# A pool of small tiles opened first, and the low parts of one product loaded into seven stage buffers

## The chip, the cores and the metric

The kernel runs on one core of a Trainium2 chip. The metric is the device time of one execution in microseconds (us). TensorE (PE in the profile) does the matmuls; VectorE (DVE), ScalarE (ACT) and GpSimd (POOL) do the element-wise work; SyncE (SP) issues most loads. DMA transfers are issued by SP, ACT and POOL.

## The reference

Two layers of a decoder trunk on 1024 tokens of width 1024, all in float32. In each layer a normalised input goes through one input projection of 3072 columns, whose parts feed a causal depthwise convolution of 31 taps (512 channels) and a retention of 4 heads; their outputs, side by side, go through the output projection `w_out` and are added to the residual. Then comes the squared-ReLU MLP (1024 to 4096 and back), then a gated per-layer input:

```
for i in range(DEPTH):
    z = rms_norm(x, norm_mix_g[i]) @ w_in[i]
    ...
    mix = jnp.concatenate([conv_out, ret_out], axis=-1) @ w_out[i]
    x = x + mix
    h = rms_norm(x, norm_ffn_g[i])
    x = x + jnp.square(jax.nn.relu(h @ w_ff1[i])) @ w_ff2[i]
    h = rms_norm(x, norm_ple_g[i])
    x = x + jax.nn.sigmoid(h @ w_ple_gate[i]) * (p[i] @ w_ple_proj[i])
return rms_norm(x, final_norm_g)
```

## The kernel before

The residual x lies transposed in SBUF for the whole run, in the pool `const`: 8 blocks of 128 channels by 2 halves of 512 tokens. Half 0 and half 1 of the tokens go through most products one after the other.

Every product is done in three matmuls (`mm3`, L252 to L254). A float32 number is split into a high part, cast by ACT to the type that TensorE takes whole (L220), and a low part, the remainder by DVE (L221); the product is high by high, high by low, low by high. So each weight tile (128 x 1024, 512 KB) exists as a `stage` tile (as loaded, by SP at L225), a `w_hi` and a `w_lo` tile, each of these pools with two buffers. `gemm` runs over eight blocks of 128 channels, 24 matmuls of 512 columns for one weight tile. The matmul's moving operand is the activation (high or low part, in `h`, `hx`, `form` or `pp`), its weights are 128 columns of `w_hi`, `w_lo` or, in the MLP's paired products, of `s_hi`, `s_lo`.

The weights of the input and output projection are used twice, once for each half. At the first use the low part is also stored to DRAM (`low_...`, L246), and at the second it is loaded back by SP into `w_lo` (L240) rather than computed again; only the cast to `w_hi` (L241) is left of the split.

The place that the change speaks of is the start of the MLP's part in each layer, which is where the output product of half 1 runs. There the code opens pools over the memory that the convolution's pools have left: `at`, `hx`, `s_hi` and `s_lo` with two buffers each, and inside them `ft` with seven. Then, in program order:

- seven fillers (`PRE` = 7, `ff1_half`): half-products of the first MLP matrix for half 0, which give PE work while the convolution of half 1 ends. Each copies a PSUM tile into an `at` buffer (ACT L602), adds the second half-product (DVE L605), applies ReLU and square (ACT L606, L607) and stores the tile to DRAM (`early`, issued by ACT at L608). An `at` buffer is free again when its store has landed;
- `w_out` of half 1 for output blocks 0 to 3, eight blocks in all, each with one weight tile whose low part was kept;
- sums and splits for the first paired MLP product (`ff1_sums`, `ff1_parts`: loads into `stage`, then DVE L588 to L591 into two `ft` buffers, ACT L220 and DVE L221 into `s_hi` and `s_lo`);
- `w_out` for blocks 4 to 7, then the norm of half 1 (`norm_forms`), which needs all of them, and which takes `ft` buffers again.

After these the paired products of the first MLP matrix run (530 to 750 us in layer 0, 1702 to 1925 us in layer 1), then those of the second (756 to 1030 and 1932 to 2200 us). A Winograd-like form is used there: sums of weight blocks are the weights, in `s_hi` and `s_lo`, and sums of activations the moving operand.

The order of the instructions on each engine is set by the tile framework's scheduler, which takes program order with priorities (`background` moves work in the order). The framework also places the pools: a pool's buffers lie at one address in all 128 partitions, one pool behind the other in the order in which they are opened; pools opened inside a `with` are given back when it ends and others take their place. The wait that a reused buffer brings is put in by the framework.

Of the kernel before, what the change touches and what calls it, by code (L numbers as in the profile page):

```python
# [13 lines left out]
F32R = mybir.dt.float32r  # L14
# [4 lines left out]
P = 128  # L19
D = 1024  # L20
# [3 lines left out]
HT = 512  # L24
# [48 lines left out]
class _Trunk:  # L73
    def __init__(self, ctx, tc, x, xT, pT, pos, wts, vecs, convw, tabs, outT):
        self.tc, self.nc = tc, tc.nc
        self.x_tok, self.xT, self.pT, self.pos, self.wts = x, xT, pT, pos, wts
        self.vecs, self.convw, self.tabs, self.outT = vecs, convw, tabs, outT
        pool = lambda name, bufs, **kw: ctx.enter_context(tc.tile_pool(name=name, bufs=bufs, **kw))
        psum = bass.MemoryType.PSUM
        self.const = pool("const", 1)  # L80
        self.pools = {
            "stage": pool("stage", 2),
            "w_hi": pool("w_hi", 2),
            "w_lo": pool("w_lo", 2),
            "h": pool("h", 8),
            "tmp": pool("tmp", 2),
            "small": pool("small", 3),
            "ps_mm": pool("ps_mm", 5, space=psum),
            "ps_ret": pool("ps_ret", 2, space=psum),
            "ps_aux": pool("ps_aux", 1, space=psum),  # L90
        }

        self.small([P, 1], "pad")
        self.right = ctx.enter_context(ExitStack())
        self.norm_pools()
        self.dram = pool("dram", 1, space=bass.MemoryType.DRAM)
        self.low = {}
# [130 lines left out]
    def weight(self, L, t):  # L228
        first = bool(self.next_weights)
        st = self.next_weights.pop(0) if first else self.stage_weight(L, t)  # L230
        hi, lo = self.tile("w_hi", D, F32R), self.tile("w_lo", D, F32R)
        kept = self.low.get((L, t))
        with ExitStack() as order:
            if first:
                for ins in self.gates.pop(0):
                    order.enter_context(self.tc.issue_after(ins))
            else:
                order.enter_context(self.background(-URGENT))
            if kept is not None:
                self.nc.sync.dma_start(out=lo.bitcast(F32), in_=kept)  # L240
                self.nc.scalar.copy(hi, st)  # L241
            else:
                self.split(st, hi, lo)
        if t < T_FF1 and kept is None:
            kept = self.dram.tile([P, D], F32, name=f"low_{L}_{t}")
            self.nc.gpsimd.dma_start(out=kept, in_=lo.bitcast(F32))  # L246
            self.low[L, t] = kept
        return hi, lo
# [344 lines left out]
    def block(self, p):  # L593
        return 4 * (p // 2) + p % 2

    def ff1_half(self, L, p, hs, early, w=None):
        nc = self.nc
        w = w or self.weight(L, T_FF1 + self.block(p))
        t = self.ft("at")
        n = KB // 2  # L600
        ps = self.gemm(w, (hs[0][:n], hs[1][:n]))
        nc.scalar.copy(t[:, 0, :], ps)  # L602
        ps = self.gemm(w, (hs[0][n:], hs[1][n:]), n)
        r = t[:, 1, :]
        nc.vector.tensor_add(r, ps, t[:, 0, :])  # L605
        nc.scalar.activation(r, r, AF.Relu)  # L606
        nc.scalar.activation(r, r, AF.Square)  # L607
        nc.scalar.dma_start(out=early[p // 2][:, p % 2], in_=t)  # L608
# [256 lines left out]
    def run(self):  # L865
# [8 lines left out]
        for L in range(DEPTH):  # L874
# [12 lines left out]
            with self.stage_pools(gen=16, conv_acc=4, ret=4, ctmp=3, rtmp=2, u=3):  # L887
                if L > 0:
                    norm_b()
                hs = h1[0]  # L890
# [18 lines left out]
                hs = h1[1]  # L909
# [10 lines left out]
                kept = self.dram.tile([P, KB, HT], F32, name=f"kept_{L}")  # L920
                h2 = self.norm(0, v0 + V_FFN, 0, True, keep=kept)
# [5 lines left out]
            early = [self.dram.tile([P, 2, 2, HT], F32, name=f"early_{L}_{j}") for j in range(NFB)]  # L927
# [23 lines left out]
            with self.stage_pools(at=2, hx=2, s_hi=2, s_lo=2):  # L951
                with self.stage_pools(ft=7):
                    for p in range(PRE):
                        self.ff1_half(L, p, h2, early)
                    mix = (mB[0] + rB[0], mB[1] + rB[1])
                    self.w_out(L, 1, mix, range(4))
                    with self.background(-URGENT):
                        fa, fb, _ = self.ff1_sums(L, 0)
                        sa, sb = self.ff1_parts(fa), self.ff1_parts(fb)
                    self.w_out(L, 1, mix, range(4, KB))  # L960
                    t2, t1 = rB[2], mB[2]
                    t3 = [self.pools["hx"].tile([P, 4, HT], F32R, name="hx") for _ in range(2)]
                    late = self.norm_forms(1, v0 + V_FFN, SLACK, kept, t1, t2, t3)
                    e = self.early_load(0, early, "tmp")
                    for p in range(PRE, NPAIR - 1):
                        self.ff1_half(L, p, h2, early)
                    w = self.weight(L, T_FF1 + self.block(NPAIR - 1))
                    raw = self.tile("stage", D)[:, HT:]
                    nc.sync.dma_start(out=raw, in_=self.wts[L * NTILES + T_FF1 + self.block(0) + 2, :, HT:])
                    with self.background(-URGENT):  # L970
                        ws = self.ff1_plain(raw), sa, sb
                    self.ff1_half(L, NPAIR - 1, h2, early, w)
                    q22, t4 = (h2[2][0], h2[3][0]), (h2[2][1], h2[3][1])
                    for f, i in ((q22, 0), (t4, 1)):
                        for item in late:
                            self.split(item[i], *item[2](f))
                    now = ws, e
                    self.ring = [*t2, *t1, t3[0], *q22, t3[1], None, *t4]
                    self.turn, self.coming = 0, []
                    for p in range(NPAIR):  # L980
                        now = self.ff1_pair(L, p, (t1, t2, t3, t4, q22), *now, early, forms, hook)
                with self.stage_pools(form=1, acc=2):
                    self.ring[8] = self.pools["form"].tile([P, 4, HT], F32R, name="form")
                    f = self.ff2_pairs(L, sources)
                    self.norm_pools()
                    self.merge_pairs(0)
                    self.ff2(L, NFB - 1, 0, f[:2])
                    self.merge_pairs(1)
                    h3A = self.norm(0, v0 + V_PLE, SLACK)
                    self.ff2(L, NFB - 1, 1, f[2:])  # L990
# [94 lines left out]
```

## Time and profile before

| | |
|---|---|
| median of 3 runs | 2378.33 us (2377.74 to 2378.8) |
| the profiled execution's own time | 2378.69 us |
| its span, first to last instruction | 2376.7 us |
| mean granted TensorE clock | 0.994 |
| PE busy | 2314.1 us, 97% of the span, 10548 matmuls |
| DVE busy | 1857.8 us, 78% |
| ACT busy | 1267.6 us, 53% |
| DMA | 403.29 MB, 170 GB/s mean |

PE busy is the union of the matmuls' times from issue to the modelled end, and consecutive matmuls overlap: a 512-column matmul is shown with some 390 ns, while the next one starts some 230 ns after it. PE's pace in a stage without idle time is therefore read from the start times in the timeline, not from the mean duration. In a timeline the square brackets behind a row give the time that the engine stood idle before it and what ended that time.

### The profile page before, as it was taken

To read this page: it belongs to the slowest core of one execution; us is meant where nothing else is said; L and a number is where in the kernel's file an instruction comes from. 1 tells how busy PE (TensorE), PEld (TensorE's weight loads), DVE (VectorE), ACT (ScalarE), POOL (GpSimd) and SP (SyncE) were. 2 spreads that over 40 slices of the span, in tenths; PEclk is the share of its full clock that TensorE was granted. 3 is DMA by queue.
4 is the path that set the end of the run, shared out by engine and by line. 5 is a ranking of instruction groups with operands and counts; after the bars stand their busy time and mean duration, and the time that the engine had idled before them with its cause. 6 is when DMAs were issued, how large, how long until landed. Compare 5 with 4: busy or idle time off the path is not lost.

```text
span 2376.7 us, 29537 instructions
## 1 busy us (share of the span) xinstructions
PE 2314.1 (97%) x10548; PEld 1886.0 (79%) x10548; DVE 1857.8 (78%) x3262; ACT 1267.6 (53%) x2090; POOL 231.9 (10%) x364
## 2 busy tenths in 40 slices
PE   8999999999999999999999999999999999999998
PEld 7887887778887878788888888777788877777887
DVE  8999997376666677878999889845766667777788
ACT  5335237365556676736542352464655567676454
POOL 1000011001221101000000100100022111010000
PEclk9999999999999999999999999999999999999999
DMA  7644544666666444422265454555566654343324
GB/s 271 194 160 150 172 149 163 227 199 204 219 233 239 141 151 138 155 72 88 89 195 180 149 171 156 175 196 187 191 218 233 237 194 164 126 162 120 89 80 151
DMA packets 119171, 403.29 MB, mean 170 GB/s; under 512 B 13216, under 2 KB 21408, under 8 KB 119024
## 3 DMA queue, kind: packets, MB, share of 16 engines
q1 hardware_dynamic: 64032, 220.75, 30.5%
q0 software_dynamic: 43472, 157.59, 18.6%
q10 hardware_dynamic: 11520, 23.07, 2.6%
q8 instruction: 82, 1.34, 0.2%
q14 instruction: 65, 0.53, 0.1%
HBM read 295.46 MB, written 105.91 MB: 169 GB/s over the span
## 4 chain that ended last, share of the span: by engine, by line
PE 63%; issue 20%; DVE 8%; DMA 3%; POOL 3%; ACT 3%; POOLq 0%; DVEq 0%; ACTq 0%
PE ps_mm L252 19%; PE ps_mm L253 19%; PE ps_mm L254 19%; DVE conv_acc L411 2%; PE ps_ret L252 2%; PE ps_ret L254 2%; PE ps_ret L253 2%; POOL h L712 1%; DMA stage<-in_wts_dram 1%; DVE w_lo L221 1%; DVE h L221 1%; POOL gn_rs L546 1%; DMA w_lo<-low 1%; DMA h<-forms 1%; DVE ntmp L277 0%
## 5 line engine op out<-in xcount | busy, mean ns | idle before, releaser
L252 PE MATMUL ps_mm<-h,w_hi 128*128 128x512 f32 (+1 forms) x1584 | 615.2, 388 | 8.6 <-ACT w_hi L241 4.2
L254 PE MATMUL ps_mm<-h,w_lo 128*128 128x512 f32 (+1 forms) x1584 | 611.5, 386 | 2.9 <-DMA w_lo<-low 2.7
L253 PE MATMUL ps_mm<-h,w_hi 128*128 128x512 f32 (+1 forms) x1584 | 613.0, 387 | 0.0
L220 ACT CAST w_hi<-stage 128x1024 fp32r<-128x1024 f32 (+2 forms) x240 | 226.6, 944 | 300.1 <-PE ps_mm L253 169.7
L252 PEld LDWEIGHTS ps_mm<-h,w_hi 128*128 128x128 f32 x1584 | 299.2, 189 | 69.3 <-ACT w_hi L241 6.1
L254 PEld LDWEIGHTS ps_mm<-h,w_lo 128*128 128x128 f32 x1584 | 299.3, 189 | 62.8 <-DMA w_lo<-low 3.5
L253 PEld LDWEIGHTS ps_mm<-h,w_hi 128*128 128x128 f32 x1584 | 299.6, 189 | 56.1
L411 DVE SCALAR_TENSOR_TENSOR conv_acc<-u,cw,conv_acc 128x512 f32<-128x512 f32 x480 | 334.6, 746 | 0.9
L221 DVE TENSOR_TENSOR w_lo<-stage,w_hi 128x1024 fp32r<-128x1024 f32 (+2 forms) x240 | 261.1, 1088 | 51.0 <-ACT w_hi L220 50.3
L252 PE MATMUL ps_mm<-h,s_hi 128*128 128x512 f32 x400 | 158.9, 397 | 4.5 <-ACT ps_mm L661 4.5
L253 PE MATMUL ps_mm<-h,s_hi 128*128 128x512 f32 x400 | 158.5, 396 | 0.0
L254 PE MATMUL ps_mm<-h,s_lo 128*128 128x512 f32 x400 | 158.0, 395 | 0.0
L252 PE MATMUL ps_mm<-w_hi,h 128*128 128x512 f32 x384 | 150.6, 392 | 0.0
L253 PE MATMUL ps_mm<-w_lo,h 128*128 128x512 f32 x384 | 150.3, 391 | 0.0
L254 PE MATMUL ps_mm<-w_hi,h 128*128 128x512 f32 x384 | 150.2, 391 | 0.0
L241 ACT CAST w_hi<-stage 128x1024 fp32r<-128x1024 f32 x64 | 67.5, 1054 | 154.4 <-PE ps_mm L253 80.7
L270 ACT ACTIVATE ntmp<-x 128x256 f32<-128x256 f32 x208 | 81.1, 413 | 84.7 <-DVE ntmp L277 32.2
L252 PE MATMUL ps_ret<-h,s_hi 128*128 128x512 f32 x272 | 110.0, 405 | 16.5 <-ACT ps_mm L744 14.4
L221 DVE TENSOR_TENSOR s_lo<-ft,s_hi 128x1024 fp32r<-128x1024 f32 x64 | 78.4, 1225 | 52.7 <-ACT s_hi L220 52.7
L221 DVE TENSOR_TENSOR h<-h 128x1024 fp32r<-128x1024 f32 x76 | 92.6, 1222 | 30.8 <-ACT h L220 30.4
L254 PE MATMUL ps_ret<-h,s_lo 128*128 128x512 f32 x272 | 108.4, 398 | 0.0
L253 PE MATMUL ps_ret<-h,s_hi 128*128 128x512 f32 x272 | 108.0, 397 | 0.0
(267 smaller groups left out, 4310.1 us busy)
## 6 DMA issues: line engine op xcount, KB each, us to landing
stage<-in_wts_dram SPq DMA_DIRECT2D x336, 512.0 KB, 4.2
forms<-ft POOLq DMA_DIRECT2D x88, 512.0 KB, 6.2
low<-w_lo POOLq DMA_DIRECT2D x64, 512.0 KB, 5.2
w_lo<-low SPq DMA_DIRECT2D x64, 512.0 KB, 3.3
h<-forms POOLq DMA_DIRECT2D x62, 512.0 KB, 6.0
early<-at ACTq DMA_DIRECT2D x32, 512.0 KB, 4.4
at<-early POOLq DMA_DIRECT2D x30, 512.0 KB, 4.2
hx<-forms POOLq DMA_DIRECT2D x18, 512.0 KB, 5.7
```

The lines of the kernel that those rows point to most:

```text
L220: self.nc.scalar.copy(hi, src)
L221: self.nc.vector.tensor_sub(lo, src, hi.bitcast(F32))
L241: self.nc.scalar.copy(hi, st)
L252: mm(ps, lhsT=wh, rhs=xh, start=start, stop=False)
L253: mm(ps, lhsT=wh, rhs=xl, start=False, stop=False)
L254: mm(ps, lhsT=wl, rhs=xh, start=False, stop=stop)
L270: square = lambda k, out: nc.scalar.activation(out, self.x[k][h][:, cs], AF.Square)
L411: nc.vector.scalar_tensor_tensor(acc, u[:, j:j + HT], w(j), acc, ALU.mult, ALU.add)
L546: nc.gpsimd.tensor_tensor(rs, rs, self.npow[:, 0:HEADS], ALU.pow)
L712: self.nc.gpsimd.dma_start(out=f[1].bitcast(F32), in_=src)
```

## The change

Four edits:

- the pool `small` (three buffers of 1032 bytes per partition and some single tiles) is opened before `stage`, `w_hi`, `w_lo`, `h` and `tmp`, and no longer behind them;
- in `weight()`, a weight tile with a kept low part takes its low part's buffer from `ft` if that pool is open, else from `w_lo` as before. `ft` is open at `w_out` of half 1 only, eight tiles in each layer;
- `ff1_half` gets the pool of its tile as an argument;
- the seven fillers take their tile from `at`, `at`, `hx`, `hx`, `at`, `at`, `hx`. `hx` has the same buffer size, and is otherwise first used behind `w_out`.

```
+            "small": pool("small", 3),
             "stage": pool("stage", 2),
             "w_hi": pool("w_hi", 2),
             "w_lo": pool("w_lo", 2),
             "h": pool("h", 8),
             "tmp": pool("tmp", 2),
-            "small": pool("small", 3),
...
-        hi, lo = self.tile("w_hi", D, F32R), self.tile("w_lo", D, F32R)
         kept = self.low.get((L, t))
+        hi = self.tile("w_hi", D, F32R)
+        if kept is not None and "ft" in self.pools:
+            lo = self.pools["ft"].tile([P, 2, HT], F32R, name="ft").rearrange("p a b -> p (a b)")
+        else:
+            lo = self.tile("w_lo", D, F32R)
...
-    def ff1_half(self, L, p, hs, early, w=None):
+    def ff1_half(self, L, p, hs, early, w=None, pool="at"):
...
-        t = self.ft("at")
+        t = self.ft(pool)
...
-                        self.ff1_half(L, p, h2, early)
+                        self.ff1_half(L, p, h2, early, pool="at" if p % 4 < 2 else "hx")
```

The first edit changes addresses. In the two built programs the pools start at these bytes of a partition:

| pool | before | remainder by 512 | after | remainder by 512 |
|---|---|---|---|---|
| `stage` | 57728 | 384 | 58880 | 0 |
| `w_hi` | 65920 | 384 | 67072 | 0 |
| `w_lo` | 74112 | 384 | 75264 | 0 |
| `h` | 82304 | 384 | 83456 | 0 |
| `tmp` | 147840 | 384 | 148992 | 0 |
| `small` | 152032 | 480 | 57824 | 480 |
| `at`, `pp` | 153088 | 0 | 153088 | 0 |
| `hx` | 161280 | 0 | 161280 | 0 |
| `s_hi` | 177664 | 0 | 177664 | 0 |
| `s_lo` | 185856 | 0 | 185856 | 0 |
| `ft`, `form` | 194048 | 0 | 194048 | 0 |

Every buffer of these pools but `small` is a multiple of 512 bytes long, so that the remainder holds for all buffers of a pool.

The order of PE's instructions is the same in both programs. On SP's queue the loads around `w_out` of half 1 change places. In layer 0, before, with `low_24` to `low_31` the kept low parts of the eight output weights and `stage` the loads of whole weight tiles (the nine ahead of `low_24` are the fillers', and the first two of `w_out`):

```order
L225 DMA stage<-in_wts_dram 128x1024 x9
L240 DMA w_lo<-low_24_2884 128x1024
L225 DMA stage<-in_wts_dram 128x1024
L240 DMA w_lo<-low_25_2918 128x1024
L225 DMA stage<-in_wts_dram 128x1024
L240 DMA w_lo<-low_26_2952 128x1024
L225 DMA stage<-in_wts_dram 128x1024
L240 DMA w_lo<-low_27_2986 128x1024
L225 DMA stage<-in_wts_dram 128x1024
L240 DMA w_lo<-low_28_3020 128x1024
L225 DMA stage<-in_wts_dram 128x1024 x2
```

The same place after:

```order
L226 DMA stage<-in_wts_dram 128x1024 x7
L245 DMA ft<-low_24_2884 128x1024
L245 DMA ft<-low_25_2918 128x1024
L226 DMA stage<-in_wts_dram 128x1024
L245 DMA ft<-low_26_2952 128x1024
L226 DMA stage<-in_wts_dram 128x1024
L245 DMA ft<-low_27_2986 128x1024
L226 DMA stage<-in_wts_dram 128x1024 x4
L245 DMA ft<-low_28_3020 128x1024
L245 DMA ft<-low_29_3054 128x1024
```

The low parts of blocks 0 and 1 (`low_24`, `low_25`) now stand ahead of the `stage` loads of both blocks, which are the single rows before `low_26` and `low_27`; before, `low_24` stood behind these two. `low_26` and `low_27` stand three `stage` loads earlier than before, `low_28` where it stood.

On ACT, the end of the fillers in layer 0, before (fillers count from 0; `early_2` takes the tiles of fillers 4 and 5):

```order
L608 DMA early_1_3742<-at 128x1024
L606 ACTIVATE at<-at 128x512
L607 ACTIVATE at<-at 128x512
L608 DMA early_2_3743<-at 128x1024
L602 COPY at<-ps_mm 128x512
L241 CAST w_hi<-stage 128x1024
L606 ACTIVATE at<-at 128x512
L602 COPY at<-ps_mm 128x512
L607 ACTIVATE at<-at 128x512
L608 DMA early_2_3743<-at 128x1024
L241 CAST w_hi<-stage 128x1024
```

And after:

```order
L613 DMA early_1_3742<-hx 128x1024
L611 ACTIVATE at<-at 128x512
L607 COPY at<-ps_mm 128x512
L612 ACTIVATE at<-at 128x512
L613 DMA early_2_3743<-at 128x1024
L246 CAST w_hi<-stage 128x1024
L611 ACTIVATE at<-at 128x512
L607 COPY hx<-ps_mm 128x512
L612 ACTIVATE at<-at 128x512
L613 DMA early_2_3743<-at 128x1024
L246 CAST w_hi<-stage 128x1024
L611 ACTIVATE hx<-hx 128x512
```

The copy of filler 5 (`L607 COPY at`) now stands ahead of the store of filler 4, and the rows are otherwise the same with other buffers: the cast of the first `w_out` weight (`L246`) keeps its place behind the copy and the store.

## Rows read from the trace of the kernel before

**Rows 1.** Busy time, share of the span and instruction count of each engine, from the page.

```profile
PE 2314.1 (97%) x10548; PEld 1886.0 (79%) x10548; DVE 1857.8 (78%) x3262; ACT 1267.6 (53%) x2090; POOL 231.9 (10%) x364
```

**Rows 2.** Windows: the stretch in us, its length, busy time of PE, PEld, DVE, ACT and POOL with the count of instructions in brackets, the granted TensorE clock, the share of the DMA engines, GB/s.

```profile
420.00:425.00 5.00, 2.86 (x12) 1.75 (x11) 1.38 (x2) 2.90 (x6) 0.00 (x0) 1.00 0.94 335
445.00:450.00 5.00, 3.44 (x15) 2.54 (x14) 1.93 (x3) 2.41 (x3) 0.00 (x0) 1.00 0.85 275
525.00:530.00 5.00, 4.58 (x12) 3.34 (x12) 3.56 (x5) 1.13 (x3) 0.54 (x1) 0.66 0.72 253
540.00:750.00 210.00, 210.00 (x908) 170.40 (x908) 139.07 (x198) 118.62 (x179) 43.27 (x65) 1.00 0.68 229
760.00:1030.00 270.00, 266.36 (x1144) 214.35 (x1143) 202.56 (x290) 180.32 (x264) 24.04 (x43) 1.00 0.43 141
1695.00:1700.00 5.00, 2.61 (x11) 1.99 (x11) 5.00 (x6) 3.13 (x5) 0.00 (x0) 1.00 0.62 214
```

**Rows 3.** Timeline of PE: the matmuls behind an idle time at the output product of half 1, layer 0 and layer 1. Start, duration, then the idle time before it and what ended it.

```profile
424.02 0.50 PE L254 MATMUL ps_mm<-h,w_lo 128*128 128x512 f32 x1 [2.00 <-DMA w_lo<-low]
...
447.17 0.50 PE L252 MATMUL ps_mm<-h,w_hi 128*128 128x512 f32 x1 [1.56 <-ACT w_hi L241]
...
1601.51 0.50 PE L254 MATMUL ps_mm<-h,w_lo 128*128 128x512 f32 x1 [0.69 <-DMA w_lo<-low]
...
1619.09 0.50 PE L252 MATMUL ps_mm<-h,w_hi 128*128 128x512 f32 x1 [1.42 <-ACT w_hi L241]
```

**Rows 4.** Timeline of ACT at the end of the fillers and the start of `w_out` of half 1, layer 0; `ACTq` is the issue of a DMA.

```profile
411.12 0.33 ACTq L608 DMA_DIRECT2D early<-at  x1
...
413.25 0.35 ACTq L608 DMA_DIRECT2D early<-at  x1
419.70 0.59 ACT L602 COPY at<-ps_mm 128x512 f32<-128x512 f32 x1 [6.48 <-DMA early<-at]
420.19 1.05 ACT L241 CAST w_hi<-stage 128x1024 fp32r<-128x1024 f32 x1
...
423.41 0.58 ACT L602 COPY at<-ps_mm 128x512 f32<-128x512 f32 x1 [1.65 <-DMA early<-at]
```

**Rows 5.** Timeline of SP's issues in the same place and around the second of PE's gaps.

```profile
415.73 0.33 SPq L240 DMA_DIRECT2D w_lo<-low  x1
...
440.21 0.33 SPq L240 DMA_DIRECT2D w_lo<-low  x1
441.51 2.13 SPq L225 DMA_DIRECT2D stage<-in_wts_dram  x2
```

**Rows 6.** Timeline of DVE: the last split of the convolution's output, layer 0.

```profile
408.64 0.69 DVE L221 TENSOR_TENSOR h<-ctmp,h 128x512 fp32r<-128x512 f32 x1 [0.69 <-ACT h L220]
```

**Rows 7.** DMA issues of the page, the loads of whole weight tiles: tile, queue, count, KB each, median us from issue to landing.

```profile
stage<-in_wts_dram SPq DMA_DIRECT2D x336, 512.0 KB, 4.2
```

**Rows 8.** Groups of the page: matmuls that move `h` against weights in `s_hi`; busy us, mean ns, idle before.

```profile
L252 PE MATMUL ps_mm<-h,s_hi 128*128 128x512 f32 x400 | 158.9, 397 | 4.5 <-ACT ps_mm L661 4.5
...
L252 PE MATMUL ps_ret<-h,s_hi 128*128 128x512 f32 x272 | 110.0, 405 | 16.5 <-ACT ps_mm L744 14.4
```

**Rows 9.** Matmuls by form with `hx` moved against weights in `w_hi`: count, shortest, median and longest duration in ns, first and last start.

```profile
L252 PE MATMUL ps_mm<-hx,w_hi x64: 388/393/628, 760.8 to 2246.5; 128*128 128x512 f32 x64
...
L252 PE MATMUL ps_ret<-hx,w_hi x16: 390/393/395, 793.0 to 1993.4; 128*128 128x512 f32 x16
```

**Rows 10.** The same for `form` moved against `w_hi`.

```profile
L252 PE MATMUL ps_mm<-form,w_hi x32: 390/392/404, 1055.9 to 2247.9; 128*128 128x512 f32 x32
```

**Rows 11.** The same for `pp` moved against `w_hi`.

```profile
L252 PE MATMUL ps_mm<-pp,w_hi x64: 388/392/404, 1077.4 to 2270.4; 128*128 128x512 f32 x64
```

**Rows 12.** Timeline of PE: first matmul of products that follow one another without idle time, in the paired products of layer 0's first and second MLP matrix, and at 1077 us in the per-layer input's product.

```profile
558.85 0.39 PE L252 MATMUL ps_mm<-hx,s_hi 128*128 128x512 f32 x1
...
561.59 0.40 PE L252 MATMUL ps_mm<-h,s_hi 128*128 128x512 f32 x1
...
564.38 0.40 PE L252 MATMUL ps_mm<-h,w_hi 128*128 128x512 f32 x1
...
567.15 0.40 PE L252 MATMUL ps_mm<-h,s_hi 128*128 128x512 f32 x1
...
884.47 0.40 PE L252 MATMUL ps_mm<-h,s_hi 128*128 128x512 f32 x1
...
888.66 0.39 PE L252 MATMUL ps_mm<-h,w_hi 128*128 128x512 f32 x1
...
891.39 0.39 PE L252 MATMUL ps_ret<-hx,s_hi 128*128 128x512 f32 x1
...
1077.42 0.40 PE L252 MATMUL ps_mm<-pp,w_hi 128*128 128x512 f32 x1
...
1099.80 0.40 PE L252 MATMUL ps_mm<-h,w_hi 128*128 128x512 f32 x1
```

## The prediction

> **What bounds the kernel now.** I read the busy times first. PE is busy for 2314.1 us of a span of 2376.7, DVE for 1857.8 and ACT for 1267.6 [rows 1]: PE is the bound, and the kernel can get shorter in two ways only, by PE standing idle less or by PE taking less time for one matmul. Then the windows: through the paired products of the first MLP matrix PE has no idle time at all (210.00 of 210.00 us), through those of the second 1.3% (266.36 of 270.00) [rows 2]. What one matmul takes there goes almost whole into the end. At the output product of half 1, on the other hand, two windows of 5 us have PE busy for 2.86 and 3.44 us [rows 2].
>
> The PE timeline says what ended these gaps: in layer 0 2.00 us for the loaded low part of the first output weight and 1.56 us for the cast of a weight, in layer 1 0.69 and 1.42 us for the same two [rows 3], 5.67 us in all. Last I looked at the starts of products that follow one another without a gap, as the durations shown (388 to 405 ns) overlap and say little. These starts are not alike. In the paired products of layer 0, 12 matmuls that move `hx` against `s_hi` and `s_lo` take from 558.85 to 561.59, 2.74 us or 228.3 ns each; the next 12, which move `h` against the same kind of weights, take 2.79 us, 232.5 ns; the next 12, `h` against `w_hi` and `w_lo`, 2.77 us, 230.8 ns. At 884.47 18 matmuls of `h` against `s_hi` take 4.19 us, 232.8 ns, the 12 of `h` against `w_hi` behind them 2.73 us, 227.5 ns. From 1077.42 to 1099.80 the 96 of `pp` against `w_hi` take 233.1 ns each [rows 12].
>
> What the products above 232 ns share is neither the moved tile nor the weights, as both occur in the quicker products too. Set beside the table of addresses, it is the remainder by 512 bytes: `h` and `w_hi` (384, 384) and `hx` and `s_hi` (0, 0) are quick, `h` and `s_hi` (384, 0) and `pp` and `w_hi` (0, 384) are not. Mean of the three products with equal remainders 228.9 ns, of the three with unequal ones 232.8: 3.9 ns.
>
> **Small pool first: the addresses.** The edit adds and removes no instruction. It puts `w_hi`, `w_lo`, `h` and `tmp` on remainder 0, where the other pools already are, so that every product has equal remainders. Which matmuls gain: `h` against `s_hi` and `s_lo`, 400 + 272 per line and three lines, 2016 [rows 8]; `hx` against `w_hi`, 64 + 16 per line, 240 [rows 9]; `form`, 32 per line, 96 [rows 10]; `pp`, 64 per line, 192 [rows 11]. Together 2544, times 3.9 ns is 10.0 us. The smallest difference between the two kinds in rows 12 is 232.5 - 230.8 = 1.7 ns, which gives 4.3 us, the largest 233.1 - 227.5 = 5.6 ns, 14.2 us. I take the mean of all six, and of its 10.0 us nine tenths, 9.0, as nearly all of these matmuls stand where PE is busy for 98.7 to 100% of the time, and the rest meets waits for others.
>
> The Trainium skill speaks against this term ("TensorE: Matmul & The Clock Gate", "Step-by-step: what each phase is for"): TensorE has two independent SBUF read ports, so that loading the next weights takes no bandwidth from the running matmul. By it the address of the weights could not matter to the matmul, and the edit would bring nothing. The starts at 558.85 and 561.59, 228.3 against 232.5 ns with the same kind of weights, do not fit it; that it is the addresses, and not something else that these products share, the trace of one layout can't show.
>
> **Low parts through `ft`, fillers over four buffers.** Instructions stay the same in number, eight loads per layer take another buffer. Two waits go.
>
> First gap (2.00 us). The low part of the first output weight is issued at 415.73 [rows 5], because a `w_lo` buffer is free only behind the fillers, and PE waits for it until 424.02. ACT stands idle for 6.48 us until 419.70 for the store of an `at` buffer that was issued at 411.12, and again 1.65 us until 423.41 for the one issued at 413.25 [rows 4], so that the cast of that weight begins at 420.19. With four buffers the copies of fillers 5 and 6 (counted from 0) find a free tile; with `ft` the low part waits for no product, but for the memory under it: the last split of the convolution's output reads `ctmp` there and ends at 408.64 + 0.69 = 409.3 [rows 6]. SP's queue then holds `low_24`, `low_25` and only then the `stage` load of the first output weight, which was free to go before. What is late next is that load. Ahead of it or beside it are two low parts, itself, one load of the kept residual for the norm and the stores of fillers 2 to 4: seven of 512 KB, 3.67 MB; at the 335 GB/s of the fullest window [rows 2] that is 11 us from 409.3, landing at 420.3, or at 418.7 if the residual's load comes behind. The cast takes 1.05 us [rows 4], so `w_hi` stands between 419.8 and 421.4; PE comes for it at 424.02 less the 2.00 us of idle time and some 0.7 us for the two matmuls ahead of the waiting one, 421.3. The cover is thin: I count the gap as gone, and 0.1 us of it left where the load comes last. If all ten transfers of that stretch (5.2 MB, 15.6 us) landed ahead of the weight, `w_hi` would come at 426.1, and PE would wait 2.8 us longer than it does now in a layer.
>
> Second gap (1.56 us). There each `stage` load stands behind a low part on SP's queue that itself waits for a `w_lo` buffer: low at 440.21, `stage` at 441.51 [rows 5], a load that takes 4.2 us in the median [rows 7] and, with the cast, ends near the 447.17 at which PE goes on. After the change four low parts are loaded before, and the `stage` loads go when their own buffer is free. Both gaps of layer 1 have the same cause and go the same way.
>
> So 5.67 us goes at best, a loss of about 2 us stands at the other end (two late weights, second gaps gone). I take 4.8: all four gaps, less the half microsecond of the thin cover in one layer and a few tenths of waits behind. Nothing hides this gain: PE runs on without a gap from here (210 of 210).
>
> What the loads in `ft` delay: `norm_forms` takes `ft` again behind `w_out`, when the last output weight's product releases it; that norm waits for these products anyway. The DMA queues carry the same bytes.
>
> **Clock.** In the window 525 to 530 the granted clock is 0.66, in 1695 to 1700, the same place of layer 1, 1.00, although PE is busy for 2.61 of 5 us there and for 4.58 in the other [rows 2]. One such stretch costs (1 - 0.66) x 5 = 1.7 us. A shifted schedule may bring one or take one away; I sum it as nothing and keep 1.7 us on either side.
>
> **Sum.** Profiled execution 2378.69 us (the span and 2.0 us around it); less 9.0, less 4.8, is 2364.9. The median of the runs is 0.36 us lower, so 2364.5. With the bounds of the terms and the clock: from 2378.3 - 14.2 - 5.7 - 1.7 = 2356.7 to 2378.3 - 4.3 + 2 + 1.7 = 2377.7. Less than 0.2%, 4.8 us, can't be told from no change.
>
> **Rivals.**
>
> 1. The addresses do not matter, and the products above 232 ns take longer for another reason (DVE and DMA are busier beside them, or the long chains of partial sums). For it: only one layout was seen, and `h` against `w_hi` at 564.38 is with 230.8 ns halfway between. Against it: products of both kinds take turns within 3 us of the same stage [rows 12]. It is also what the rule of the Trainium skill above would make of the edit. Then only the gaps go: 2378.3 - 4.8 = 2373.5, just at the edge of what can be told.
>
> 2. Remainder 0 is itself the slower one. Up to 10548 - 2544, about 8000 matmuls [rows 1], go from (384, 384) to (0, 0). Rows 12 have 227.5 and 230.8 ns for the first pair and 228.3 for the second, so that nothing is sure to a nanosecond; the largest price that they allow is 230.8 - 227.5 = 3.3 ns. At 13.8 / 8000 = 1.7 ns the whole gain is eaten, from there the kernel is slower; at 2.6 ns it ends at 2378.3 - 13.8 + 20.8 = 2385. Against it: 228.3 lies between the other two, as a product with equal remainders should.
>
> 3. The gaps do not go: the weight behind two low parts is late, and the wait for the low part becomes one for the cast. Then 2378.3 - 9.0 is 2369.3, with one clock stretch more 2371.0.
>
> **Chances.** Forecast (both terms) 0.68, with a range of its own from 2359 to 2370; rival 1 0.14, of which half is faster by over 0.2%; rival 3 0.13, all but a tenth of it faster; rival 2 0.05, of which four fifths slower. Faster 0.68 + 0.07 + 0.11 = 0.86, slower 0.04, same 0.10. The range, 2357 to 2376, takes in the low bound, rival 3 and most of rival 1.
>
> **What the profile after would show.** Addresses: products of `h` against `s_hi` and of `pp` against `w_hi` at 228 to 229 ns from start to start, and PE busy by some 10 us less; if they stay at 232, rival 1 holds; if `h` against `w_hi` in the projections goes above 229, rival 2. Gaps: no idle time of PE for `w_lo` or `ft` near 424 and 1601, and none for the cast near 447 and 1619; the low loads issued near 409; ACT no longer idle for the stores of the fillers. A PE gap for `w_hi` (L246) near 422 would be rival 3.

## The result and the profile after

The changed kernel takes 2360.03 us (median of 4 runs, 2358.13 to 2361.93) against 2378.51 of the kernel before beside it: ratio 0.9923, 95% interval 0.9906 to 0.994, 18.5 us less. It lies 4.5 us below the forecast of 2364.5, inside the range. A second time, beside the last experiments, it was 2358.89 against 2379.15, 0.9909 (0.9895 to 0.9923).

The page of the changed kernel: busy times, three groups of matmuls with the idle time before them, and the loads of low parts.

```profile
PE 2297.2 (97%) x10548; PEld 1886.0 (80%) x10548; DVE 1857.1 (79%) x3262; ACT 1266.6 (54%) x2090; POOL 231.8 (10%) x364
...
L257 PE MATMUL ps_mm<-h,w_hi 128*128 128x512 f32 (+1 forms) x1584 | 613.8, 388 | 5.3 <-ACT w_hi L221 3.9
...
L259 PE MATMUL ps_mm<-h,w_lo 128*128 128x512 f32 (+1 forms) x1456 | 560.7, 385 | 0.2
...
L257 PE MATMUL ps_mm<-h,s_hi 128*128 128x512 f32 x400 | 156.9, 392 | 4.8 <-ACT ps_mm L666 4.8
...
w_lo<-low SPq DMA_DIRECT2D x48, 512.0 KB, 3.3
```

PE is busy for 16.9 us less than in [rows 1] with the same 10548 matmuls, and the span is 19.9 us shorter, so that 3.0 us of idle time went as well in this profile. The matmuls against `w_lo` have lost their wait for a load; 48 low parts still go to `w_lo`, the other 16 to `ft`.

PE's timeline, first matmuls of the products that answer to those of [rows 12]:

```profile
553.85 0.39 PE L257 MATMUL ps_mm<-hx,s_hi 128*128 128x512 f32 x1
...
556.57 0.39 PE L257 MATMUL ps_mm<-h,s_hi 128*128 128x512 f32 x1
...
559.29 0.39 PE L257 MATMUL ps_mm<-h,w_hi 128*128 128x512 f32 x1
...
562.01 0.39 PE L257 MATMUL ps_mm<-h,s_hi 128*128 128x512 f32 x1
...
1077.19 0.39 PE L257 MATMUL ps_mm<-pp,w_hi 128*128 128x512 f32 x1
...
1079.23 0.39 PE L257 MATMUL ps_mm<-pp,w_hi 128*128 128x512 f32 x1
```

Each 12 matmuls take 2.72 us, 226.7 ns, whichever pair it is: `hx` against `s_hi`, `h` against `s_hi`, `h` against `w_hi`; nine of `pp` against `w_hi` take 2.04 us, 226.7 ns. Before it was 228.3, 232.5, 230.8 and 233.1 ns. So the unequal pairs got quicker, and the equal ones too.

Windows at the output product of half 1, and the stage of the paired products (columns as in [rows 2]):

```profile
417.00:422.00 5.00, 5.00 (x24) 4.14 (x23) 0.69 (x1) 2.58 (x4) 0.00 (x0) 1.00 1.03 417
442.00:447.00 5.00, 4.90 (x22) 3.74 (x21) 1.19 (x3) 2.04 (x3) 0.75 (x1) 1.00 1.00 315
530.00:740.00 210.00, 209.24 (x923) 172.90 (x922) 140.51 (x200) 120.13 (x182) 43.22 (x65) 1.00 0.66 225
```

The windows that had PE busy for 2.86 and 3.44 of 5 us are full or nearly so. ACT and SP there, the counterparts of [rows 4] and [rows 5]:

```profile
413.10 0.59 ACT L607 COPY at<-ps_mm 128x512 f32<-128x512 f32 x1 [0.92 <-PE ps_mm L259]
...
414.25 0.33 ACTq L613 DMA_DIRECT2D early<-at  x1
417.69 1.05 ACT L246 CAST w_hi<-stage 128x1024 fp32r<-128x1024 f32 x1 [3.47 <-DMA stage<-in_wts_dram]
418.65 0.62 ACT L611 ACTIVATE at<-at 128x512 f32<-128x512 f32 x1
419.18 0.57 ACT L607 COPY hx<-ps_mm 128x512 f32<-128x512 f32 x1
...
422.80 1.05 ACT L246 CAST w_hi<-stage 128x1024 fp32r<-128x1024 f32 x1 [2.53 <-DMA stage<-in_wts_dram]
```

```profile
409.03 0.80 SPq L245 DMA_DIRECT2D ft<-low  x2
410.47 0.33 SPq L226 DMA_DIRECT2D stage<-in_wts_dram  x1
```

ACT waits for the `stage` load instead of for the fillers' stores, and the cast begins at 417.69, before PE wants it. SP issues the first two low parts at 409.03, where the last split of the convolution's output has just let go of the memory.

### The profile page after: what moved, and what is told of

It reads as the page before. It is cut to its first block, busy times and chain, and to the rows that moved or that the text cites. A ratio compares the mean times of both kernels' runs of the same rounds, so it can differ in the third digit from the quotient of the medians.

```text
span 2356.8 us, 29538 instructions
## 1 busy us (share of the span) xinstructions
PE 2297.2 (97%) x10548; PEld 1886.0 (80%) x10548; DVE 1857.1 (79%) x3262; ACT 1266.6 (54%) x2090; POOL 231.8 (10%) x364
## 3 DMA queue, kind: packets, MB, share of 16 engines
q0 software_dynamic: 43472, 157.59, 18.5%
## 4 chain that ended last, share of the span: by engine, by line
PE 66%; issue 18%; DVE 8%; DMA 3%; ACT 3%; POOL 2%; POOLq 0%; DVEq 0%; ACTq 0%
PE ps_mm L257 19%; PE ps_mm L258 19%; PE ps_mm L259 19%; DVE conv_acc L416 2%; PE ps_ret L257 2%; PE ps_ret L259 2%; PE ps_ret L258 2%; DVE w_lo L222 1%; POOL h L717 1%; POOL gn_rs L551 1%; DMA stage<-in_wts_dram 1%; DVE h L222 1%; DMA h<-forms 1%; ACT w_hi L221 0%; DVE ntmp L282 0%
## 5 line engine op out<-in xcount | busy, mean ns | idle before, releaser
L259 PE MATMUL ps_mm<-h,w_lo 128*128 128x512 f32 (+1 forms) x1456 | 560.7, 385 | 0.2
L259 PEld LDWEIGHTS ps_mm<-h,w_lo 128*128 128x128 f32 x1456 | 275.0, 189 | 53.1 <-DVE w_lo L222 1.3
L222 DVE TENSOR_TENSOR w_lo<-stage,w_hi 128x1024 fp32r<-128x1024 f32 (+2 forms) x240 | 260.7, 1086 | 48.5 <-ACT w_hi L221 48.0
L246 ACT CAST w_hi<-stage 128x1024 fp32r<-128x1024 f32 x64 | 67.5, 1054 | 159.3 <-PE ps_mm L258 67.5
L222 DVE TENSOR_TENSOR h<-h 128x1024 fp32r<-128x1024 f32 x76 | 92.6, 1222 | 34.2 <-ACT h L221 33.9
L222 DVE TENSOR_TENSOR s_lo<-ft,s_hi 128x1024 fp32r<-128x1024 f32 x64 | 78.4, 1225 | 49.4 <-ACT s_hi L221 49.4
```

Source lines behind the costliest of these rows:

```text
L222: self.nc.vector.tensor_sub(lo, src, hi.bitcast(F32))
L259: mm(ps, lhsT=wl, rhs=xh, start=False, stop=stop)
```

## The experiments

Times are medians beside runs of the kernel before on the same chip, whose own median there was 2379 to 2382 us; what is compared is the ratio. The chips differ by some us, so differences of less than 2 us between comparisons are not read.

### The small pool alone, and the other edits alone

```
+            "small": pool("small", 3),
             "stage": pool("stage", 2),
...
             "tmp": pool("tmp", 2),
-            "small": pool("small", 3),
```

> The kernel before with the pool small opened first, nothing else. Theory (equal remainders by 512 let a matmul follow in 227 ns, unequal ones in 232.7, and the products behind an unequal one need some matmuls to come back to 227): PE busy falls by about 17 us to 2297, the time by 13 to 14 us, to 2364 to 2366 us; the gaps of PE at 424 and 447 us stay (2.0 and 1.6 us). Rival (the remainders do not matter, the quicker matmuls of the changed kernel come from the other edits): 2378 us, products of h against s_hi stay at 232.5 ns.

The second is the changed kernel with this edit taken back:

```
-            "small": pool("small", 3),
...
             "tmp": pool("tmp", 2),
+            "small": pool("small", 3),
```

> The changed kernel with the pool small back behind tmp: the kernel before with the low parts through ft and the fillers over four buffers. Theory: the four gaps go, 6 us, 2372 to 2373 us, and matmuls of h against s_hi stay at 232.5 ns. Rival (the gaps are worth little by themselves, and the 18 us are the addresses' alone): 2377 to 2378 us.

Small alone: 2364.86 against 2382.08, 0.9927 (0.9911 to 0.9943), 17.2 us. The others alone: 2375.96 against 2382.08, 0.9975 (0.9966 to 0.9984), 6.1 us. Both theories hold, the addresses with more than was expected. PE's longest waits from 410 to 450 us with small alone (waiting, releaser, us in all, times, longest):

```profile
PE ps_mm L254 <- DMA w_lo<-low: 2.0, 1, 2.0
PE ps_mm L252 <- ACT w_hi L241: 1.7, 1, 1.7
PE ps_mm L252 <- ACT w_hi L220: 1.1, 1, 1.1
```

The gaps stand as before, 2.0 and 1.7 us, while PE's pace is that of the changed kernel (227.0 ns, in the table further down): the two terms have separate causes. In the second kernel the waits for `w_lo` and for the cast of `w_hi` (L246) are gone from both layers, and PE busy is 2319.2 us, not lower than before (the mean granted clock of this profile is 0.992, that of the kernel before's 0.994).

### Low parts and fillers apart

```
-        if kept is not None and "ft" in self.pools:
+        if False:
```

> The changed kernel with the low parts back in w_lo: small first and the fillers over four buffers. Theory (the low part's late load is what PE waits for first, the fillers' buffers only what ACT waits for): the gaps stay to a few tenths, 2364 to 2366 us as small alone. Rival (ACT's wait for the stores is the cause): most of the 6 us goes, 2360 to 2361 us.

```
-                        self.ff1_half(L, p, h2, early, pool="at" if p % 4 < 2 else "hx")
+                        self.ff1_half(L, p, h2, early)
```

> The changed kernel with all seven fillers back in at: small first and the low parts through ft. Theory: the low parts are there, the cast of the first output weight comes behind ACT's wait for the store of filler 3, at 420.2 us at the earliest and later by what two more loads take from the stores; a gap of 0 to 2 us stays in layer 0, 2360 to 2362 us. Rival (the four filler buffers do the most): 2364 to 2366 us.

Small and the fillers: 2365.28 us, 0.9931 (0.9918 to 0.9945), as small alone. Small and the low parts: 2360.02 us, 0.9908 (0.9892 to 0.9923), as the changed kernel. The profile of the first (fillers only), PE's waits from 410 to 450 us:

```profile
PE ps_mm L259 <- DMA w_lo<-low: 2.4, 1, 2.4
PE ps_mm L257 <- ACT w_hi L246: 1.3, 1, 1.3
```

ACT is not held by the stores there, it casts the first output weight at 416.58, and still PE waits 2.4 us for the low part: ACT's 6.48 us of idle time in [rows 4] lay beside a longer wait. The other way round, with the low parts alone, ACT is held for 5.68 us by the store of a filler, and PE does not wait at this place: it comes for the first output weight at 421.97, behind the cast.

```profile
419.89 0.59 ACT L607 COPY at<-ps_mm 128x512 f32<-128x512 f32 x1 [5.68 <-DMA early<-at]
420.37 1.05 ACT L246 CAST w_hi<-stage 128x1024 fp32r<-128x1024 f32 x1
```

A gap for a cast is left in this kernel, 2.1 us in layer 0:

```profile
445.95 0.50 PE L257 MATMUL ps_mm<-h,w_hi 128*128 128x512 f32 x1 [2.06 <-ACT w_hi L246]
```

By that, and by 1.1 us in layer 1, the filler buffers seemed worth some 3 us, which the times did not show. But both stand at the fifth output weight, that of layer 0 some 25 us behind the place where the filler buffers act. So the three were run side by side once more:

> The changed kernel again, side by side with the next two. Theory (the two terms add): 18 us below the kernel before, and 4 to 6 us below small alone. Rival (what the gaps gave at the output product is given back by other waits): within 2 us of small alone.

> Small first and the low parts through ft, all fillers in at, again. Theory (by the first profile two gaps for the cast, 2.1 and 1.1 us, are left, which the four filler buffers take away): 2 to 3 us above the changed kernel. Rival (the filler buffers are worth nothing): the same time within 1 us.

> Small first alone, again. Theory: 13 to 14 us below the kernel before, 4 to 6 us above the changed kernel. Rival (small is the whole effect): within 1 us of the changed kernel.

The changed kernel 2358.89 us (0.9909, interval 0.9895 to 0.9923), low parts only 2358.95 (0.9916, 0.9902 to 0.993), small alone 2364.47 (0.9938, 0.9925 to 0.9951), before 2379.15. The low parts bring 5.5 us over small alone, the fillers' buffers 0.1 us, which can't be told from nothing (the five times of each kernel spread over 4 to 5 us): the theory that I had formed on one profile fell. Why is seen in the changed kernel's own second profile, where the gap is back, on PE and ACT:

```profile
444.64 0.50 PE L257 MATMUL ps_mm<-h,w_hi 128*128 128x512 f32 x1 [1.74 <-ACT w_hi L246]
```

```profile
439.73 1.04 ACT L221 CAST s_hi<-ft 128x1024 fp32r<-128x1024 f32 x1
443.55 1.04 ACT L246 CAST w_hi<-stage 128x1024 fp32r<-128x1024 f32 x1 [2.78 <-DMA stage<-in_wts_dram]
```

And the same place in its first profile, where it is not:

```profile
439.57 1.03 ACT L221 CAST s_hi<-ft 128x1024 fp32r<-128x1024 f32 x1
441.52 1.05 ACT L246 CAST w_hi<-stage 128x1024 fp32r<-128x1024 f32 x1 [0.92 <-DMA stage<-in_wts_dram]
```

The cast waits for the `stage` load of the fifth output weight. SP issues that load at 437.69 in the one and 437.85 in the other execution, and a low part 0.42 us behind it in both; in the one it is there at about 441.5, in the other at 443.5. Its first part lands 3.0 us after the issue in both; it is the last parts that are late. One program, two outcomes of one transfer among others: the gap of 1.7 us is not bound to the filler buffers. What held the last parts up is not shown.

### The sums behind the output product

```
-                    self.w_out(L, 1, mix, range(4))
+                    self.w_out(L, 1, mix)
                     with self.background(-URGENT):
                         fa, fb, _ = self.ff1_sums(L, 0)
                         sa, sb = self.ff1_parts(fa), self.ff1_parts(fb)
-                    self.w_out(L, 1, mix, range(4, KB))
```

> The changed kernel with the sums and splits for the first paired product put behind all eight blocks of w_out of half 1, so that their two stage loads are not between those of w_out. Theory (the gap at 443 us is there when the stage load of the fifth output weight, issued between two low parts, lands late): no gap of PE in the whole of w_out in either layer, 1 to 2 us below the changed kernel where that has the gap, 2357 to 2359 us. Rival (the sums are late for the first paired product, or the norm of half 1 is slowed by them): a new wait of PE near 470 to 525 us, 2359 us or more.

2359.78 us against 2380.18, 0.9916 (0.9903 to 0.9929): the changed kernel's time. The gap at 443 us is not there in its profile, and waits of 0.5 us for `w_lo` (L222) and 0.3 us for `ntmp` came near 465 us. Each theory is seen in part, and what they come to together can't be told from no effect.

### Which addresses

All on the kernel before, with bytes put ahead of the pools of the MLP and of the per-layer input (384, 128 or 416):

```
+    @contextmanager
+    def gap(self):
+        with self.tc.tile_pool(name="gap", bufs=1) as gap:
+            gap.tile([P, 96], F32, name="gap")
+            yield
...
-            with self.stage_pools(at=2, hx=2, s_hi=2, s_lo=2):
+            with self.gap(), self.stage_pools(at=2, hx=2, s_hi=2, s_lo=2):
...
-            with self.stage_pools(pp=8, pr=16):
+            with self.gap(), self.stage_pools(pp=8, pr=16):
```

> The kernel before with a gap of 384 bytes ahead of the pools of the MLP and of the per-layer input, so that all tiles that TensorE reads there have the remainder 384 by 512 (and different ones by 1024). Theory (equal remainders by 512 count): products at 227 ns throughout these stages, PE busy 2297 us, 2364 to 2366 us. Rival A (a multiple of 512 is what counts, so that the kernel before was held back by its tiles at 384): no gain or a loss, 2378 us or more. Rival B (remainders by a larger power of two count): 2378 us.

> The same with a gap of 128 bytes: remainders 384 and 128, 256 apart by 512. Theory (equality by 512): unequal, as slow as before, products of h against s_hi at 232 to 233 ns, 2378 us. Rival (equality by 256 is enough): 227 ns and 2364 to 2366 us.

> The same with a gap of 416 bytes: remainders 384 and 416, only 32 apart. If only exact equality by 512 counts: 232 to 233 ns and 2378 us. If the price grows with the distance: a quarter of it at 32 of 128 bytes, 228 to 229 ns and some 2368 to 2370 us.

The last is the changed kernel with 128 bytes ahead of `s_hi`:

```
-            with self.stage_pools(at=2, hx=2, s_hi=2, s_lo=2):
+            with self.stage_pools(at=2, hx=2), self.gap(), self.stage_pools(s_hi=2, s_lo=2):
```

> The changed kernel with a gap of 128 bytes between hx and s_hi: s_hi, s_lo, ft, form and acc at remainder 128, everything else at 0. Theory (moved tile against weights): h and hx against s_hi at 232 to 233 ns, form against s_hi (128, 128) at 227, h against w_hi in the projections at 227, and the 2016 + 672 + 96 unequal matmuls cost 16 us: 2375 to 2377 us. Rival (what slows PE is another engine reading and writing at another remainder): the products of hx against w_hi and pp against w_hi slow as well, or no difference between the pairs.

| kernel | remainders by 512: `h` and `w_hi`, `hx` and `pp`, `s_hi` and `form` | ratio to before, interval | unequal pairs, ns | equal pairs in these stages, ns |
|---|---|---|---|---|
| before | 384, 0, 0 | | 232.6 | 228.6 |
| changed | 0, 0, 0 | 0.9923 (0.9906 to 0.994) | | 227.0 |
| small alone | 0, 0, 0 | 0.9927 (0.9911 to 0.9943) | | 227.0 |
| all at 384 | 384, 384, 384 | 0.9929 (0.9908 to 0.995) | | 227.0 |
| 256 apart | 384, 128, 128 | 0.9944 (0.9927 to 0.996) | 227.0 | 226.9 |
| 32 apart | 384, 416, 416 | 0.9994 (0.9982 to 1.0006) | 233.2 | 228.5 |
| changed, `s_hi` at 128 | 0, 0, 128 | 0.9984 (0.9973 to 0.9994) | 232.6 | 227.9 |

The two columns of ns are means of the time from a matmul's start to the next one's, over all neighbouring matmuls of 512 columns in the trace with less than 300 ns between them (2500 unequal ones in the kernel before, 2700 equal ones in the stages of the MLP and the per-layer input), sorted by the address of the moved tile against that of the next weights.

All at 384: no multiple of 512 is needed, equality is; rival A falls, and rival B too, since by 1024 these addresses differ. 256 apart: the theory said 232 to 233 ns, and it is 227.0, so equality by 256 is enough; here the rival was right. The first matmuls of three products there, `h` against `s_hi`, `h` against `w_hi`, `h` against `s_hi`:

```profile
563.41 0.39 PE L258 MATMUL ps_mm<-h,s_hi 128*128 128x512 f32 x1
...
566.13 0.39 PE L258 MATMUL ps_mm<-h,w_hi 128*128 128x512 f32 x1
...
568.85 0.39 PE L258 MATMUL ps_mm<-h,s_hi 128*128 128x512 f32 x1
```

2.72 us for 12, as after the change, though the remainders by 512 are 384 and 128 in the first. 32 apart, `h` against `s_hi` twice, then `hx` against `s_hi`:

```profile
565.37 0.39 PE L258 MATMUL ps_mm<-h,s_hi 128*128 128x512 f32 x1
...
568.16 0.40 PE L258 MATMUL ps_ret<-h,s_hi 128*128 128x512 f32 x1
...
570.96 0.40 PE L258 MATMUL ps_mm<-hx,s_hi 128*128 128x512 f32 x1
...
573.69 0.40 PE L258 MATMUL ps_mm<-h,s_hi 128*128 128x512 f32 x1
```

2.79, 2.80 and 2.73 us: 32 bytes cost as much as 128, so the price does not grow from the one distance to the other. `s_hi` at 128 in the changed kernel, `h`, `h` and `hx` against `s_hi`:

```profile
564.01 0.40 PE L263 MATMUL ps_mm<-h,s_hi 128*128 128x512 f32 x1
...
566.80 0.39 PE L263 MATMUL ps_ret<-h,s_hi 128*128 128x512 f32 x1
...
569.59 0.39 PE L263 MATMUL ps_mm<-hx,s_hi 128*128 128x512 f32 x1
...
572.38 0.40 PE L263 MATMUL ps_mm<-h,s_hi 128*128 128x512 f32 x1
```

2.79 us for each: `hx` against `s_hi`, the quickest pair of the kernel before, is as late as the others once the weights are moved by 128 bytes, and `pp` against `w_hi`, which nothing moved, keeps 226.7 ns (36 matmuls from 1078.93 to 1087.09 us). `hx` against `w_hi`, unequal in the kernel before (232.7 ns in the mean of the trace) and equal here, is at 229.1: the rival, by which it would stay slow, falls. It is the pair that counts. Its median, 2375.61 against 2381.54, is what the theory said, and near what the other edits give without the small pool.

That left the equal pairs of the kernel before, which were at 228.6 and not at 227. Its timeline, two products that follow an unequal one, `hx` against `s_hi` from 586.61 and `h` against `w_hi` from 592.14:

```profile
586.61 0.39 PE L252 MATMUL ps_mm<-hx,s_hi 128*128 128x512 f32 x1
...
587.76 0.39 PE L254 MATMUL ps_mm<-hx,s_lo 128*128 128x512 f32 x1
...
589.35 0.40 PE L252 MATMUL ps_mm<-h,s_hi 128*128 128x512 f32 x1
...
592.14 0.40 PE L252 MATMUL ps_mm<-h,w_hi 128*128 128x512 f32 x1
...
593.53 0.40 PE L252 MATMUL ps_mm<-h,w_hi 128*128 128x512 f32 x1
...
594.67 0.40 PE L254 MATMUL ps_mm<-h,w_lo 128*128 128x512 f32 x1
```

The first five matmuls of the one take 1.15 us, 230 ns each, the other seven 1.59 us, 227.1; the first six of the next 1.39 us, 231.7, the five after them 1.14 us, 228. In the mean of the whole trace the first three equal matmuls behind an unequal one take 230 to 231 ns, the next six 228 to 230, and from the tenth on it is 227; at the same places of the changed kernel it is 227 from the first on. The lateness of an unequal product is carried into the first half or more of the equal one behind it. With no unequal product left there is nothing to carry.

## Why the prediction was right, and where its sizes were off

**What bounds the kernel.** Right: PE's pace and PE's gaps were the two ways, and each edit acted on one of them alone.

**Addresses: right in kind, too small in size.** 9.0 us were taken, between 4.3 and 14.2; small alone measured 17.2 and 14.7 us in its two comparisons, and PE's busy time fell by 16.9 in the first profile of the changed kernel and by 19.4, to 2294.7, in the second. The mis-sized step is "Mean of the three products with equal remainders 228.9 ns, of the three with unequal ones 232.8: 3.9 ns". The equal products were taken as a measure of an undisturbed pace, and they were not one: the first half of each still ran late. By the table, the unequal pairs win 5.6 ns, 2513 times, 14.1 us, and the equal ones of these stages 1.6 ns, 2704 times, 4.3 us, together 18.4. The second term was not in the sum at all, and the upper bound, which compared the six products only, missed it too. The halfway product at 564.38 (230.8 ns), which I gave to rival 1, was the sign of it.

**Rivals 1 and 2.** Rival 1 falls with small alone: no other edit, 17.2 us. Rival 2 falls with the changed kernel and with all at 384, both 227.0 ns. The Trainium skill's rule of two independent read ports ("TensorE: Matmul & The Clock Gate", "Step-by-step: what each phase is for") would have made the edit worth nothing; what was drawn from it, that the weights' address can't matter to the running matmul, does not hold here, 233.2 ns at 32 bytes apart against 227.0.

**Low parts and fillers.** 4.8 us were taken, 6.1 and 5.6 measured. First gap: right, and with more room than forecast, as the `stage` load was there by 417.69, when the cast begins, and not between 418.7 and 420.3. Rival 3, by which the first weight is late and PE waits for its cast, did not come: no profile with the low parts in `ft` has such a wait at the first weight. But the fillers' four buffers, which the text put beside the low parts as a second wait that goes, are worth 0.1 us: ACT's idle time was not on the path, as the run with the low parts alone shows, where it is there without a wait of PE. Second gap: the step "the `stage` loads go when their own buffer is free" is right by SP's queue and does not settle the gap: the load took 3.7 us in one profile of the changed kernel and 5.6 in the other, with the same low part issued 0.42 us behind it, and the gap was away in the one and there, with 1.74 us, in the other.

**What was given back.** The sum let a tenth of the pace meet waits for others, and of the gaps the text said that nothing hides them. PE's idle time, the span less its busy time, is 62.6 us before, 65.9 and 66.1 in the two profiles of small alone, and 59.6 and 63.0 in those of the changed kernel. So a quicker PE alone gives 3.3 to 3.5 us of its pace back as waits, nearer a fifth than a tenth; 1.4 of them come at the second matrix's products, which wait for ACT (L744) for 18.3 us in place of 16.9. In the first profile of the changed kernel 6.1 us between matmul starts are gone at the four gaps, and its idle time is only 3.0 us less than before; in the second, with its gap of 1.74 us, it is no less than before. In the times of the second comparison the terms add up all the same: 14.7 us of small alone and 5.6 of the other edits are the 20.3 of both. The first has 17.2 and 6.1, with 18.5 for both, from another comparison, and their intervals overlap.

**Clock.** It was summed as nothing, with 1.7 us on either side for one stretch. The stretches of the lower clock (1.2 in place of 2.4 GHz) move more than that from one execution of a kernel to the next. In the first profile of the changed kernel, columns as in [rows 2]:

```profile
520.00:525.00 5.00, 4.00 (x11) 3.17 (x12) 4.14 (x6) 1.54 (x3) 0.54 (x1) 0.66 0.74 253
1680.00:1685.00 5.00, 2.57 (x12) 1.83 (x11) 5.00 (x7) 3.75 (x7) 0.55 (x1) 1.00 0.44 152
1685.00:1690.00 5.00, 4.29 (x13) 2.77 (x12) 2.97 (x4) 1.78 (x3) 0.54 (x1) 0.66 0.66 209
2105.00:2115.00 10.00, 7.80 (x27) 5.97 (x26) 7.62 (x12) 7.80 (x11) 0.53 (x1) 0.83 0.51 194
```

The same kernel in its second profile:

```profile
520.00:525.00 5.00, 2.62 (x11) 1.82 (x11) 5.00 (x7) 3.17 (x5) 0.47 (x1) 1.00 0.59 207
1685.00:1690.00 5.00, 4.29 (x12) 2.90 (x10) 2.81 (x4) 1.28 (x3) 0.54 (x1) 0.66 0.68 229
```

The stretch that [rows 2] show at 525 is still there in the first profile, some 4 us earlier like everything around it, and two more stand in layer 1, one behind 5 us in which PE was busy for 2.57. By the prediction's reckoning each costs 1.7 us, so the first profile carries some 3.4 us that the kernel before's does not (mean granted clock 0.992 against 0.994). In the second the stretch in layer 0 is away, although PE was busy for 2.62 of 5 us there, and the one at 2105 too (mean 0.994). The PE busy times of the two profiles, 2297.2 and 2294.7 us, differ the same way, and so do the times of runs of one kernel: in the second comparison the changed kernel took 2354.84 us in the run with a mean clock of 0.996 and 2359.96 in one with 0.994.

## What to carry to other kernels

Where weights and moved tiles alternate without a gap, read the time from one matmul's start to the next per pair of tiles, and set it beside the addresses: on this kernel a pair that is 32 or 128 bytes off by 256 costs 6 ns of 227, and one odd pool between the big ones put 2500 matmuls there. That pool is small: 1032 bytes of a partition in all its buffers together, not in each of three. Take the undisturbed pace from a stretch where nothing of the suspected kind stands near, since a late product makes the next one late too. And an idle time on an engine that is waited for is a gain only if its wait ends last: test edits that come together one by one.

## What was not expected

- Tiles whose addresses are equal by 256 bytes run at full pace: 32 bytes apart is as dear as 128 (233.2 and 232.6 ns) and 256 is free (227.0). Other distances were not tried, and why the chip does so no run here shows.
- The lateness is carried over: behind an unequal product it takes some nine matmuls until 227 ns is reached again.
- One program shows a gap of 1.74 us in one execution and none in another, by a load that takes 3.7 or 5.6 us. A profile's single gap of that size, set against a single profile without it, told the wrong thing of the filler buffers, though its place, at the fifth weight, already spoke against them.
